# Multiplying the input product by the norm's token scale after PSUM instead of before it

## The chip, the cores and the metric

One core of a Trainium2 chip. The time is the device time of one launch in microseconds (us), as the median of several runs; smaller is better. The engines work side by side, each through its own queue in order: TensorE (matmul; "PE" in the profile, "PEld" its weight loads), VectorE ("DVE"), ScalarE ("ACT"), GpSimd ("POOL") and the DMA queues of SyncE ("SPq"), ScalarE ("ACTq") and GpSimd ("POOLq").

## The reference

One layer of an encoder over a sequence of 1024 tokens of 1024 features, all fp32. Its first lines are what the change touches:

```
h = x * rsqrt(mean(x * x, over features) + 1e-6) * norm1_w     # RMS norm of each token
z = h @ w_in                                                   # 1024 x 1024 by 1024 x 4528
c_q, c_kv, k_r, gdn_qkv, ga_f, ga_b, gb_f, gb_b, gdn_gate, gate_a, gate_b = split(z)
```

From z come: a latent attention (c_q and c_kv are normed again and multiplied up to queries, keys and values), a gated delta rule in both directions (gdn_qkv passes a convolution over five neighbouring tokens and a silu; the decays are exponentials of ga and gb), and three sets of gates (silu or sigmoid of z). Then follow the merge of both branches, an output product, a second norm, a squared-ReLU MLP and a last norm.

The rsqrt of the norm is one number per token. Multiplying a token's row of x by it, or that token's column of the product by it, gives the same z.

## The kernel before

Everything is held transposed: features lie on the 128 partitions, tokens along the free dimension, 1024 of them. x is eight tiles of 128 x 1024 (xt[0] to xt[7]), and z comes in 36 tiles of 128 features x 1024 tokens, one for each block w_in[i]. Tiles 0 to 3 are the keys (step k of the code), 4 is a mix of small columns (m), 5 to 8 the values (v), 9 to 11 the latents (c), 12 to 15 the queries (q), and 16 to 35 the gates (g).

A product at full precision is done in three matmul passes on split operands. A number is split into a high part (rounded to the type fp32r) and a low part (the rest); the passes are high x high, high x low and low x high. `split` makes both parts of a tile of x (a cast on ScalarE, a subtraction on VectorE or GpSimd); `wtile` loads a block of weights and does the same (L146 the load, L148 the cast, L150 the subtraction). `mm3` issues the 48 matmuls of one z tile: for each of the eight tiles of x the passes high x high and high x low in two halves of 512 tokens, then the eight of low x high. All matmuls of these helpers have line L157.

The prologue (L207 to L258) runs so. Weight blocks 0 and 1 and x are loaded by SyncE's queue; VectorE multiplies the two blocks by norm1_w (L221). TensorE forms z tiles 0 and 1 from the plain fp32 operands, 16 fp32 matmuls each, which the profile shows as 32 records; K0 orders them by the arrival of x. ScalarE squares the tiles of x (L230), VectorE adds the squares up (L232), TensorE sums them over the partitions with a matrix of ones (L237, at high priority), and `rsqrt` makes the token scale r1 from it on ScalarE and VectorE (L187 to L192). VectorE multiplies tiles 0 and 1 by r1 while it copies them out of PSUM (L247). Then, for each k, VectorE forms x * norm1_w * r1 (L251), ScalarE casts it (L170) and VectorE or GpSimd subtracts (L171); these pairs, xs, are what the other 34 tiles are formed from.

`z_tile(i)` gives tile i in PSUM, and each step takes it from there: `conv_tile` (the steps k, v and q) multiplies and adds five shifted copies on VectorE (L277), for k straight out of PSUM, for v and q out of a copy that ScalarE makes (L270); step m and `lora_norm` copy it with ScalarE; step g applies silu or sigmoid on ScalarE (L533) and stores the result to memory with ScalarE's DMA queue (L534).

PSUM has two buffers of 128 x 1024 (psA: z tiles, the Q, K and projection products) and four of 128 x 512 (psB). SBUF units are counted: 35 large ones ("u"; the names mem.alloc), 5 for passing work ("f"; fill.alloc), three raw weight buffers, four for split weights.

The string ORDER gives the order of the steps in the program. A scheduler of the framework then orders each engine's instructions: by their place in the program, with an instruction that must wait letting a later one go ahead, all by estimated durations. The semaphores follow from it; on the chip each engine runs its list in order. The i steps of ORDER are sixteen parts of a triangular inverse on VectorE (L519 multiplies, L521 adds, each on the result of the one before); what they give is stored by SyncE (L525) and read in the z steps (L655, L661) near the end of ORDER. Q steps (L584 multiplies a product out of PSUM) stand between the gates. After ORDER comes the scan of the delta rule: its states are loaded (L707, L708), and its exponentials run on ScalarE (L754), used first at L757.

Of the kernel before, what the change touches and what calls it, by code (L numbers as in the profile page):

```python
# [46 lines left out]
K0 = 6  # L47
# [50 lines left out]
def block_kernel(ctx: ExitStack, tc: tile.TileContext, xT, pos, cpar, gpar, w_in, w_uq, w_ukv,  # L98
# [108 lines left out]
    w0, xt = [], []  # L207
    nw = par[:, N1:N1 + 8]
    for k in range(8):
        if k < 2:  # L210
            raw = wp.tile([128, 1024], F32, tag="wraw", name=f"wi{k}_r", bufs=3)
            w0.append(raw)
            w3, src = (x.rearrange("p (k c) -> p k c", k=8) for x in (raw, w_in[k]))
            parts = (slice(0, 2), slice(2, 8))
            nc.sync.dma_start(w3[:, parts[0]], src[:, parts[0]])
        xt.append(mem.alloc())
        nc.sync.dma_start(xt[k].ap, xT[k * 128:(k + 1) * 128, :])
        if k < 2:
            nc.sync.dma_start(w3[:, parts[1]], src[:, parts[1]])
            for ks in parts:  # L220
                V.tensor_tensor(w3[:, ks], w3[:, ks], bc(nw[:, ks], 128), ALU.mult)  # L221
    pz = [pa("ps_z0"), pa("ps_z1")]
    for i, k in [(i, k) for k in range(K0) for i in range(2)] + \
            [(i, k) for i in range(2) for k in range(K0, 8)]:
        mm_pass(pz[i], w0[i][:, k * 128:(k + 1) * 128], xt[k].ap, k == 0, k == 7)
    psn = [pb("ps_n1a"), pb("ps_n1b")]
    acc = fill.alloc()
    for k in range(8):
        sq = acc if k == 0 else fill.alloc()
        last = A.activation(sq.ap, xt[k].ap, AF.Square)  # L230
        if 0 < k < 7:
            V.tensor_tensor(acc.ap, acc.ap, sq.ap, ALU.add)  # L232
            sq.free()
    with tc.high_priority(1000):
        for i, t in enumerate((acc, sq)):
            for sl, ps in zip(HS, psn):
                T.matmul(ps, ones, t.ap[:, sl], start=i == 0, stop=i == 1)  # L237
    acc.free()
    sq.free()
    r1 = fill.alloc()  # L240
    for i in range(2):
        rsqrt(r1.ap[:, HS[i]], psn[i], 1.0 / D, eps_t[:, 0:1], half("m"), half("t"),
              None if i else last)
    zb = big("ZB")
    zb = [zb[:, 0:1024], zb[:, 1024:2048]]
    for ps, z in zip(pz, zb):
        V.tensor_tensor(z, ps, r1.ap, ALU.mult)  # L247
    xs = []
    for k in range(8):
        xn = fill.alloc()  # L250
        V.scalar_tensor_tensor(xn.ap, xt[k].ap, pcol(N1 + k), r1.ap, ALU.mult, ALU.mult)  # L251
        h, l = mem.pair()
        split(h, l, xn.ap, G if k % 2 else V)
        xn.free()
        xs.append((h, l))

    def z_tile(i):
        if i < 2:  # L258
            return zb[i]
# [3 lines left out]
        return ps  # L263

    def conv_tile(dst, i, ch, slow=False):

        z = z_tile(i)
        if slow:
            zt = fill.alloc()
            A.copy(zt.ap, z)  # L270
            z = zt.ap
# [7 lines left out]
        if slow:  # L279
            zt.free()  # L280
# [23 lines left out]
    def s_k(h):  # L304
# [7 lines left out]
        if h == 1:  # L312
            r1.free()
            for t in xt:
                t.free()
# [4 lines left out]
    def s_m(_):  # L320
        ps = z_tile(4)
        zm.append(mem.alloc())
        A.copy(zm[0].ap, ps)
        G.dma_start(d_misc, zm[0].ap[0:16, :])
# [174 lines left out]
    def s_v(h):  # L499
        vT[h] = mem.alloc()  # L500
        conv_tile(vT[h].ap, 5 + h, 8 + h, slow=True)
# [28 lines left out]
    def s_g(i):  # L530
        ps = z_tile(16 + i)
        t = fill.alloc()
        late[0] = A.activation(t.ap, ps, AF.Silu if i < 4 else AF.Sigmoid)  # L533
# [9 lines left out]
    def lora_norm(z0, count, dim, wcol, name):  # L543
        tiles = []
        for i in range(count):
            pz_ = z_tile(z0 + i)
            t = fill.alloc()
            A.copy(t.ap, pz_)
# [139 lines left out]
    def s_q(h):  # L688
        qT[h] = mem.alloc()
        late[0] = conv_tile(qT[h].ap, 12 + h, h, slow=True)  # L690
# [9 lines left out]
    for h, l in xs:  # L700
        h.free()
        l.free()

# [832 lines left out]
```

## Time and profile before

| what | us |
|---|---|
| median of 3 runs | 1686.58 |
| lowest, highest | 1681.42, 1687.2 |
| the profiled execution, its own time | 1683.32 |
| its span | 1681.5 |
| TensorE matmul busy, share of the span | 1608.4 (96%) |
| VectorE busy | 1231.5 (73%) |
| ScalarE busy | 815.3 (48%) |
| GpSimd busy | 224.3 (13%) |
| TensorE's mean granted clock, share of full speed | 0.984 |

The profile is of one execution; its times count from the start of the span. "Idle before" an instruction, with a releaser behind an arrow, says how long the engine had nothing to do and what ended that. A name like u<-f,u gives the tile written and the tiles read, without buffer numbers; wi_r, wi_h and wi_l are the raw, the high and the low part of a block of w_in.

### The profile page before, as it was taken

The numbers are of one execution on the slowest core, as the hardware profiler recorded it, in microseconds if no ns is written. First come the engines' busy times: TensorE is split into PE (matmuls) and PEld (weight loads), VectorE is DVE, ScalarE is ACT, GpSimd is POOL, SyncE is SP. The second block draws the span as 40 slices with busy tenths as digits, with TensorE's granted clock in tenths as the row PEclk, the third lists the DMA queues.
The fourth block names the chain that finished last, engine by engine and source line by source line (L and its number), as shares of the span: only waits on it lengthen the run. The fifth ranks groups of instructions, "written<-read, shape, count | busy, mean of one in ns | idle before, by whom it ended". The sixth has DMA issues, their size and how long they took to land.

```text
span 1681.5 us, 21862 instructions
## 1 busy us (share of the span) xinstructions
PE 1608.4 (96%) x8177; PEld 1324.0 (79%) x8177; DVE 1231.5 (73%) x1823; ACT 815.3 (48%) x1393; POOL 224.3 (13%) x247
## 2 busy tenths in 40 slices
PE   8899999999989889999999998999999889999997
PEld 3687788878768878888878886888888657888886
DVE  6987999931345678888787568677776699888766
ACT  5567431441335557878762335444444443444333
POOL 1212100000004445555300000000000000000012
PEclk9999999999989999999999999999999999999999
DMA  4135243472234252101173212443443454444213
GB/s 184 58 108 135 79 160 114 137 213 88 76 101 132 74 159 76 51 26 39 55 245 113 101 38 81 150 151 138 168 152 141 154 208 143 154 161 154 83 57 101
DMA packets 87545, 200.00 MB, mean 119 GB/s; under 512 B 20224, under 2 KB 37888, under 8 KB 87184
## 3 DMA queue, kind: packets, MB, share of 16 engines
q1 hardware_dynamic: 63840, 158.14, 28.3%
q10 hardware_dynamic: 22784, 36.97, 6.4%
q0 software_dynamic: 816, 3.51, 1.0%
q8 instruction: 64, 1.05, 0.3%
q14 instruction: 41, 0.34, 0.1%
HBM read 136.79 MB, written 61.80 MB: 118 GB/s over the span
## 4 chain that ended last, share of the span: by engine, by line
PE 77%; DVE 10%; DMA 5%; ACT 5%; issue 2%; POOL 1%; ACTq 0%; SPq 0%; DVEq 0%; POOLq 0%
PE ps_z L157 15%; PE ps_af L1200 10%; PE ps_ay L1200 9%; PE ps_cf L1200 5%; PE ps_w L157 5%; PE ps_p L157 5%; PE ps_s L849 5%; PE ps_cy L1200 4%; PE ps_pv L891 3%; PE ps_pt L872 3%; PE ps_df L1200 3%; PE ps_y L1440 2%; PE ps_dy L1200 2%; DMA f<-d_vl 2%; DVE u L277 1%
## 5 line engine op out<-in xcount | busy, mean ns | idle before, releaser
L157 PE MATMUL ps_z<-u,wi_h 128*128 128x512 f32 x1088 | 260.9, 396 | 10.5 <-POOL u L171 1.7
L157 PEld LDWEIGHTS ps_z<-u,wi_h 128*128 128x128 f32 x1088 | 204.7, 190 | 57.7 <-ACT u L170 3.9
L1200 PE MATMUL ps_af<-u,f_w 128*128 128x512 f32 x768 | 181.9, 389 | 0.0
L1200 PE MATMUL ps_ay<-u,y_w 128*128 128x512 f32 x672 | 168.2, 396 | 8.7 <-ACT y_w L1188 3.1
L1200 PEld LDWEIGHTS ps_af<-u,f_w 128*128 128x128 f32 x768 | 144.0, 188 | 30.2 <-ACT u L1241 0.4
L1200 PEld LDWEIGHTS ps_ay<-u,y_w 128*128 128x128 f32 x672 | 125.8, 189 | 42.2 <-ACT y_w L1188 5.9
L157 PE MATMUL ps_z<-u,wi_l 128*128 128x512 f32 x544 | 133.5, 395 | 0.0
L1448 POOL TENSOR_TENSOR u<-u,q 128x256 f32<-128x256 f32 x20 | 16.2, 809 | 828.0 <-ACT q L1447 827.7
L157 PEld LDWEIGHTS ps_z<-u,wi_l 128*128 128x128 f32 x544 | 102.7, 190 | 21.6
L849 PE MATMUL ps_s<-u,u 128*128 128x512 f32 x384 | 105.9, 409 | 3.5 <-ACT u L837 2.4
L1200 PE MATMUL ps_cf<-u,f_w 128*128 128x512 f32 x384 | 94.7, 397 | 5.7 <-ACT f_w L1188 5.7
L150 DVE TENSOR_TENSOR wi_l<-wi_r,wi_h 128x1024 fp32r<-128x1024 f32 x34 | 41.5, 1220 | 77.3 <-PE ps_z L157 61.3
L852 DVE TENSOR_REDUCE sx<-ps_s 128x1 f32<-128x1024 f32 x64 | 77.9, 1218 | 21.3 <-PE ps_s L849 19.9
L1200 PE MATMUL ps_cy<-u,y_w 128*128 128x512 f32 x336 | 86.1, 394 | 6.7 <-DVE y_w L1189 6.2
L1200 PEld LDWEIGHTS ps_cf<-u,f_w 128*128 128x128 f32 x384 | 73.6, 192 | 22.0 <-ACT f_w L1188 6.5
L854 ACT ACTIVATE u<-ps_s,sx 128x1024 f32<-128x1024 f32 x64 | 72.2, 1128 | 31.9 <-DVE sx L852 31.5
L148 ACT CAST wi_h<-wi_r 128x1024 fp32r<-128x1024 f32 x34 | 35.7, 1050 | 104.0 <-PE ps_z L157 89.3
L878 DVE TENSOR_TENSOR u<-ps_pt,u 128x512 fp32r<-128x512 f32 x128 | 82.3, 679 | 5.1 <-ACT u L877 5.1
L856 POOL TENSOR_SCALAR u<-u,sx 128x1024 f32<-128x1024 f32 x64 | 72.0, 1128 | 84.9 <-DVE sx L855 82.0
L1200 PEld LDWEIGHTS ps_cy<-u,y_w 128*128 128x128 f32 x336 | 62.8, 189 | 22.9 <-DVE y_w L1189 8.3
L849 PEld LDWEIGHTS ps_s<-u,u 128*128 128x128 f32 x384 | 68.2, 191 | 15.3 <-ACT u L837 2.8
L1189 DVE TENSOR_TENSOR f_w<-f_r,f_w 128x512 fp32r<-128x512 f32 x48 | 33.1, 690 | 56.6 <-ACT f_w L1188 56.6
(368 smaller groups left out, 3262.1 us busy)
## 6 DMA issues: line engine op xcount, KB each, us to landing
u<-d_u SPq DMA_DIRECT2D x42, 512.0 KB, 4.3
wi_r<-w_in SPq DMA_DIRECT2D x34, 512.0 KB, 3.5
f_r<-w_ff SPq DMA_DIRECT2D x32, 512.0 KB, 3.3
d_u<-u SPq DMA_DIRECT2D x28, 512.0 KB, 4.0
d_z<-f ACTq DMA_DIRECT2D x20, 512.0 KB, 3.2
f<-d_z SPq DMA_DIRECT2D x20, 512.0 KB, 4.3
y_r<-w_ff SPq DMA_DIRECT2D x18, 512.0 KB, 3.9
d_u<-u ACTq DMA_DIRECT2D x16, 512.0 KB, 2.6
```

Of the source, the lines that this page charges most:

```text
L148: A.copy(hi, raw)
L150: V.tensor_tensor(lo, raw, hi.bitcast(F32), ALU.subtract)
L157: T.matmul(ps[:, sl], w, x[:, sl], start=start, stop=stop)
L849: T.matmul(pss[:, sl], a.r[:, qsl], b.r[:, sl], start=i == 0, stop=i == 2)
L852: V.tensor_reduce(sx[:, 0:1], pss, AX.X, ALU.max, negate=True)
L854: A.activation(P.ap, pss, AF.Exp, bias=sx[:, 0:1], accum_out=sx[:, 1:2])
L856: G.tensor_scalar(P.ap, P.ap, sx[:, 1:2], 1.0, ALU.mult, ALU.mult)
L872: T.transpose(pt[:, k * 128:(k + 1) * 128], P.ap[:, ko:ko + 128], ident)
L878: V.tensor_tensor(lv, p3, hf_, ALU.subtract)
L891: T.matmul(pso[:, 0:256], VC[kb].r[:, h * 128:(h + 1) * 128], PT[kg][i].r[:, k * 256:(k + 1) * 256], start=kb == 0 and i == 0, stop=kb == ...
L1200: T.matmul(ps, w[:, a, k * 128:(k + 1) * 128], self.xops[k][i].parts[b], start=n == 0 and i in FIRST, stop=n == 3 * self.g - 1, skip_group ...
L1440: T.matmul(ps[:, 0:n], w[:, o:o + 128], x[:, sl], start=j + k == 0, stop=j == 2 and k == 3)
```

## The change

The token scale r1 leaves the operands. x is split as x * norm1_w: ScalarE makes the high part in one scaled copy, VectorE the low part in one multiply-and-subtract, straight from each loaded tile (the first two in halves). All 36 tiles, also 0 to 2, are formed in split passes; for tiles 0 to 2 the three passes are issued one after the other. The norm's sum is formed behind tile 1. `z_scaled` multiplies every tile by r1 on VectorE on its way out of PSUM, in one instruction (tiles 0 to 2: in two halves; tile 2 lies in two psB buffers). So `conv_tile` always works on an SBUF copy, and step g applies its activation to that copy in place. ScalarE's squares are held behind the casts (that of tile k behind the cast of tile k + 4, at most 7). The order of loads becomes w_in[0], x, w_in[1]. r1 is held in a large unit until the end of ORDER; the tiles of x are let go after their squares.

```
--- before.py
+++ after.py
@@ -44,7 +44,6 @@
 
 ORDER = "kkkmrvGGklGtvSvvGsciiSigiigcSSgiQigQQiiQgQgQigQgiQqgigoggiKVKVViKgigogigzzqggzqKqzggV"
 PIECES = tuple((i, i + 256) for i in range(0, S, 256))
-K0 = 6
 LEAD, LAG = 3, 2
 VS, VS2 = (3, 4), (0, 1)
 HQ = 0
@@ -204,71 +203,84 @@
 
 
 
-    w0, xt = [], []
-    nw = par[:, N1:N1 + 8]
+    def wraw(src, name):
+        raw = wp.tile([128, 1024], F32, tag="wraw", name=f"{name}_r", bufs=3)
+        nc.sync.dma_start(raw, src)
+        return raw
+
+    xt, xs = [], []
+    w0 = wraw(w_in[0], "wi0")
     for k in range(8):
-        if k < 2:
-            raw = wp.tile([128, 1024], F32, tag="wraw", name=f"wi{k}_r", bufs=3)
-            w0.append(raw)
-            w3, src = (x.rearrange("p (k c) -> p k c", k=8) for x in (raw, w_in[k]))
-            parts = (slice(0, 2), slice(2, 8))
-            nc.sync.dma_start(w3[:, parts[0]], src[:, parts[0]])
         xt.append(mem.alloc())
         nc.sync.dma_start(xt[k].ap, xT[k * 128:(k + 1) * 128, :])
-        if k < 2:
-            nc.sync.dma_start(w3[:, parts[1]], src[:, parts[1]])
-            for ks in parts:
-                V.tensor_tensor(w3[:, ks], w3[:, ks], bc(nw[:, ks], 128), ALU.mult)
-    pz = [pa("ps_z0"), pa("ps_z1")]
-    for i, k in [(i, k) for k in range(K0) for i in range(2)] + \
-            [(i, k) for i in range(2) for k in range(K0, 8)]:
-        mm_pass(pz[i], w0[i][:, k * 128:(k + 1) * 128], xt[k].ap, k == 0, k == 7)
-    psn = [pb("ps_n1a"), pb("ps_n1b")]
+    w1 = wraw(w_in[1], "wi1")
+
+    def wsplit(raw, name):
+        hi = wp.tile([128, 1024], F32R, tag="ws", name=f"{name}_h", bufs=4)
+        A.copy(hi, raw)
+        lo = wp.tile([128, 1024], F32R, tag="ws", name=f"{name}_l", bufs=4)
+        V.tensor_tensor(lo, raw, hi.bitcast(F32), ALU.subtract)
+        return hi, lo
+
+    early, casts = [wsplit(w0, "wi0")], []
+    for k in range(8):
+        h, l = mem.pair()
+        for sl in (HS if k < 2 else [slice(0, 1024)]):
+            cast = A.activation(h.r[:, sl], xt[k].ap[:, sl], AF.Copy, scale=pcol(N1 + k))
+            V.scalar_tensor_tensor(l.r[:, sl], xt[k].ap[:, sl], pcol(N1 + k), h.ap[:, sl],
+                                   ALU.mult, ALU.subtract)
+        xs.append((h, l))
+        casts.append(cast)
+    early.append(wsplit(w1, "wi1"))
     acc = fill.alloc()
     for k in range(8):
         sq = acc if k == 0 else fill.alloc()
         last = A.activation(sq.ap, xt[k].ap, AF.Square)
+        tc.add_manual_dep(last.ins, casts[min(k + 4, 7)].ins.name, nosync, reason="order")
+        xt[k].free()
         if 0 < k < 7:
             V.tensor_tensor(acc.ap, acc.ap, sq.ap, ALU.add)
             sq.free()
-    with tc.high_priority(1000):
-        for i, t in enumerate((acc, sq)):
-            for sl, ps in zip(HS, psn):
-                T.matmul(ps, ones, t.ap[:, sl], start=i == 0, stop=i == 1)
-    acc.free()
-    sq.free()
-    r1 = fill.alloc()
-    for i in range(2):
-        rsqrt(r1.ap[:, HS[i]], psn[i], 1.0 / D, eps_t[:, 0:1], half("m"), half("t"),
-              None if i else last)
-    zb = big("ZB")
-    zb = [zb[:, 0:1024], zb[:, 1024:2048]]
-    for ps, z in zip(pz, zb):
-        V.tensor_tensor(z, ps, r1.ap, ALU.mult)
-    xs = []
-    for k in range(8):
-        xn = fill.alloc()
-        V.scalar_tensor_tensor(xn.ap, xt[k].ap, pcol(N1 + k), r1.ap, ALU.mult, ALU.mult)
-        h, l = mem.pair()
-        split(h, l, xn.ap, G if k % 2 else V)
-        xn.free()
-        xs.append((h, l))
+    r1 = mem.alloc()
+    pz = []
+    for i in range(3):
+        w = early[i] if i < 2 else wtile(w_in[i], f"wi{i}")
+        ps = [pa(f"ps_z{i}")] if i < 2 else [pb(f"ps_z{i}a"), pb(f"ps_z{i}b")]
+        pz.append([ps[0][:, 0:HALF], ps[0][:, HALF:2 * HALF]] if i < 2 else ps)
+        for p, q in ((0, 0), (0, 1), (1, 0)):
+            for k in range(8):
+                for s, sl in enumerate(HS):
+                    T.matmul(pz[i][s], w[p][:, k * 128:(k + 1) * 128], xs[k][q].r[:, sl],
+                             start=p + q + k == 0, stop=p == 1 and k == 7)
+        if i == 1:
+            psn = [pb("ps_n1a"), pb("ps_n1b")]
+            for j, t in enumerate((acc, sq)):
+                for sl, ps in zip(HS, psn):
+                    T.matmul(ps, ones, t.ap[:, sl], start=j == 0, stop=j == 1)
+            acc.free()
+            sq.free()
+            for j in range(2):
+                rsqrt(r1.ap[:, HS[j]], psn[j], 1.0 / D, eps_t[:, 0:1], half("m"), half("t"),
+                      None if j else last)
 
     def z_tile(i):
-        if i < 2:
-            return zb[i]
+
+        if i < 3:
+            return zip(HS, pz[i])
         w = wtile(w_in[i], f"wi{i}")
         ps = pa(f"ps_z{i}")
         mm3(ps, w, 0, xs)
-        return ps
-
-    def conv_tile(dst, i, ch, slow=False):
-
-        z = z_tile(i)
-        if slow:
-            zt = fill.alloc()
-            A.copy(zt.ap, z)
-            z = zt.ap
+        return [(slice(0, 1024), ps)]
+
+    def z_scaled(dst, i):
+        for sl, ps in z_tile(i):
+            V.tensor_tensor(dst[:, sl], ps, r1.ap[:, sl], ALU.mult)
+
+    def conv_tile(dst, i, ch):
+
+        zt = fill.alloc()
+        z = zt.ap
+        z_scaled(z, i)
         c = CW + ch * 5
         A.activation(dst, z, AF.Copy, scale=pcol(c + 2))
         for t in (0, 1, 3, 4):
@@ -276,8 +288,7 @@
             d0, d1 = max(0, -o), S - max(0, o)
             V.scalar_tensor_tensor(dst[:, d0:d1], z[:, d0 + o:d1 + o], pcol(c + t),
                                    dst[:, d0:d1], ALU.mult, ALU.add)
-        if slow:
-            zt.free()
+        zt.free()
         return A.activation(dst, dst, AF.Silu)
 
 
@@ -309,18 +320,13 @@
                                accum_out=kn[:, h * N + n:h * N + n + 1])
         t.free()
         kn_last[:] = [ins]
-        if h == 1:
-            r1.free()
-            for t in xt:
-                t.free()
 
 
     zm, d_misc = [], dr.tile([16, 1024], F32, name="d_misc")
 
     def s_m(_):
-        ps = z_tile(4)
         zm.append(mem.alloc())
-        A.copy(zm[0].ap, ps)
+        z_scaled(zm[0].ap, 4)
         G.dma_start(d_misc, zm[0].ap[0:16, :])
 
 
@@ -498,7 +504,7 @@
 
     def s_v(h):
         vT[h] = mem.alloc()
-        conv_tile(vT[h].ap, 5 + h, 8 + h, slow=True)
+        conv_tile(vT[h].ap, 5 + h, 8 + h)
 
     def s_S(h):
         stack(vT[h], h, d_vs).free()
@@ -528,9 +534,9 @@
     d_z = dr.tile([20, 128, 1024], F32, name="d_z")
 
     def s_g(i):
-        ps = z_tile(16 + i)
         t = fill.alloc()
-        late[0] = A.activation(t.ap, ps, AF.Silu if i < 4 else AF.Sigmoid)
+        z_scaled(t.ap, 16 + i)
+        late[0] = A.activation(t.ap, t.ap, AF.Silu if i < 4 else AF.Sigmoid)
         A.dma_start(d_z[i], t.ap)
         t.free()
 
@@ -543,9 +549,8 @@
     def lora_norm(z0, count, dim, wcol, name):
         tiles = []
         for i in range(count):
-            pz_ = z_tile(z0 + i)
             t = fill.alloc()
-            A.copy(t.ap, pz_)
+            z_scaled(t.ap, z0 + i)
             tiles.append(t)
         ps = pa(name)
         for i, t in enumerate(tiles):
@@ -687,7 +692,7 @@
             mem.live -= 1
     def s_q(h):
         qT[h] = mem.alloc()
-        late[0] = conv_tile(qT[h].ap, 12 + h, h, slow=True)
+        late[0] = conv_tile(qT[h].ap, 12 + h, h)
 
     steps = {"k": s_k, "m": s_m, "l": s_l, "r": s_r, "G": s_G, "s": s_s, "t": s_t, "v": s_v,
              "S": s_S, "i": s_i, "g": s_g, "c": s_c, "Q": s_Q, "K": s_K, "V": s_V, "o": s_o,
@@ -700,6 +705,7 @@
     for h, l in xs:
         h.free()
         l.free()
+    r1.free()
 
 
     KST, VST = [mem.alloc() for _ in range(H)], [mem.alloc() for _ in range(H)]
```

## Rows read from the trace of the kernel before

**Rows 1.** The profile's page, busy share of each engine.

```profile
PE 1608.4 (96%) x8177; PEld 1324.0 (79%) x8177; DVE 1231.5 (73%) x1823; ACT 815.3 (48%) x1393; POOL 224.3 (13%) x247
```

**Rows 2.** Busy time (instructions) by engine and stretch; granted clock, DMA share, GB/s.

```profile
42.00:55.00 13.00, 9.84 (x34) 6.85 (x33) 13.00 (x9) 6.27 (x6) 7.23 (x3) 0.87 0.04 16
61.00:187.00 126.00, 122.71 (x587) 100.09 (x586) 105.59 (x119) 80.74 (x154) 27.04 (x29) 1.00 0.36 104
187.00:345.00 158.00, 155.60 (x689) 127.57 (x688) 154.66 (x173) 60.40 (x62) 1.03 (x2) 1.00 0.38 132
...
484.00:531.00 47.00, 42.28 (x268) 33.84 (x267) 16.47 (x15) 17.11 (x28) 4.75 (x6) 0.85 0.57 173
```

**Rows 3.** TensorE in order of time: start, us, line, operation, [idle before].

```profile
6.42 15.42 PE L157 MATMUL ps_z<-u,wi_r 128*128 128x512 f32 x30 [6.42 <-DMA u<-xT]
...
25.11 14.75 PE L157 MATMUL ps_z<-u,wi_r 128*128 128x512 f32 x34
...
57.54 3.83 PE L157 MATMUL ps_z<-u,wi_l 128*128 128x512 f32 x16
61.21 4.92 PE L157 MATMUL ps_z<-u,wi_h 128*128 128x512 f32 x21
...
72.65 7.53 PE L157 MATMUL ps_z<-u,wi_h 128*128 128x512 f32 x32 [1.12 <-DVE u L277]
...
112.14 1.17 PE L157 MATMUL ps_z<-u,wi_h 128*128 128x512 f32 x4 [1.19 <-DVE u L361]
```

**Rows 4.** ScalarE and VectorE in order of time, from the norm's sum to r1.

```profile
24.45 0.69 ACT L187 ACTIVATE f<-ps_n1a,eps_t 128x512 f32<-128x512 f32 x1 [2.75 <-PE ps_n1a L237]
...
29.98 0.69 DVE L192 SCALAR_TENSOR_TENSOR f<-t,f 128x512 f32<-128x512 f32 x1
```

**Rows 5.** A line: count, min/median/max ns, first and last start, shape.

```profile
L247 DVE TENSOR_TENSOR ZB<-ps_z,f x2: 1210/1210/1211, 39.8 to 45.4; 128x1024 f32<-128x1024 f32 x2
...
L533 ACT ACTIVATE f<-ps_z x20: 1023/1029/1031, 190.8 to 523.2; 128x1024 f32<-128x1024 f32 x20
...
L277 DVE SCALAR_TENSOR_TENSOR u<-ps_z,par,u x8: 1266/1276/1283, 66.3 to 110.7; 128x1022 f32<-128x1022 f32 x4, 128x1023 f32<-128x1023 f32 x4
```

**Rows 6.** TensorE and VectorE: a z tile, a Q tile, the next.

```profile
254.03 7.42 PE L157 MATMUL ps_z<-u,wi_h 128*128 128x512 f32 x32
...
264.91 1.98 PE L157 MATMUL ps_q<-u,wq_h 128*128 128x512 f32 x8
...
267.63 7.42 PE L157 MATMUL ps_z<-u,wi_h 128*128 128x512 f32 x32
...
255.65 1.22 DVE L584 TENSOR_TENSOR f<-ps_q,u 128x1024 f32<-128x1024 f32 x1
```

**Rows 7.** ScalarE in order of time, squares of the last two tiles of x.

```profile
17.01 1.06 ACT L230 ACTIVATE f<-u 128x1024 f32<-128x1024 f32 x1 [0.21 <-DMA u<-xT]
18.29 1.06 ACT L230 ACTIVATE f<-u 128x1024 f32<-128x1024 f32 x1 [0.22 <-DMA u<-xT]
```

**Rows 8.** The stretches again, instructions that write or read ps_z alone.

```profile
61.00:187.00 126.00, 105.85 (x458) 84.95 (x457) 10.20 (x8) 9.30 (x9) 1.00 0.36 104
187.00:345.00 158.00, 131.03 (x573) 107.11 (x572) 0.00 (x0) 13.35 (x13) 1.00 0.38 132
```

**Rows 9.** The same of line L519 alone.

```profile
187.00:345.00 158.00, 52.99 (x62) 1.00 0.38 132
```

**Rows 10.** VectorE and TensorE, the inverse's end and first reader.

```profile
344.78 0.22 DVE L521 TENSOR_TENSOR SY<-SY,f 128x62 f32<-128x62 f32 x1
...
407.42 0.24 PE L661 MATMUL ptz<-ident,f 64*64 64x64 f32 x1
```

**Rows 11.** ScalarE and VectorE, the scan's first exponentials and their first use.

```profile
527.03 2.44 ACT L754 ACTIVATE f<-f,st 128x128 f32<-128x128 f32 x8
...
531.08 0.68 DVE L757 TENSOR_TENSOR f<-f,u 128x512 f32<-128x512 f32 x1
```

**Rows 12.** TensorE in order of time, behind the late load.

```profile
498.14 0.47 PE L662 MATMUL ptz<-ident,f 64*64 64x64 f32 x2 [4.72 <-DMA f<-d_x]
```

## The prediction

> **What bounds the kernel now.** The busy shares come first: TensorE matmul 96%, VectorE 73%, ScalarE 48% [rows 1]. So a change pays only where TensorE stands idle or works longer than it must. The table by stretches says where: from 61 us to 345 us TensorE is busy 122.7 of 126 us and 155.6 of 158, but from 42 to 55 us it is busy 9.84 of 13 while VectorE is busy all 13, and from 484 to 531 us 42.28 of 47 [rows 2]. The third view is TensorE's own order of time [rows 3]. The reader sees there the prologue: z tiles 0 and 1 as plain fp32 matmuls (wi_r) from 6.42 us to 39.9 us, with the norm's sum between them (ps_n1), and tile 2, the first split one (wi_h, wi_l), whose last pass starts only at 57.54. The split rows of x are what it waits for: they need the token scale r1, ready at 30.7 us [rows 4], and then eight multiplies, eight casts and eight subtractions, half of these on GpSimd. Last, the costs of one operation of each kind [rows 5].
>
> The sum is made against the profiled execution, 1683.3 us (span 1681.5, and 1.8 around it). The median shown, 1686.6, is 3.3 us higher; I add that at the end.
>
> **The prologue, before.** One split z tile takes 10.88 us (254.03 to 264.91) [rows 6]: 48 matmuls of 0.227. The fp32 tiles have 64 records: 34 of them take 14.75 us, 0.434 each, so a tile of 32 takes 13.9; the first 30 took 15.42 [rows 3], 2.4 more than at that pace. That is the engine's slow start. Tile 2's last pass begins at 57.54 and the tile after it goes on at 61.21 with 21 of its 32 wi_h matmuls [rows 3], so 11 had been run while tile 2 waited: 11 x 0.227 = 2.5 us, and tile 2 ends "in effect" at 58.7 us.
>
> **The prologue, after.** Loads: 512 KB land every 1.28 us, and the tenth 512 KB (two weight tiles, eight of x) is there at 18.29 [rows 7]. The order becomes w0, eight of x, w1: the last tile of x is there at 17.0, the first at about 8.0 (seven loads earlier), w1 at 18.3. ScalarE casts each tile of x as it lands, about as long as a square, 1.06 us [rows 7], under the 1.28 us of a load. But squares are let in behind the fifth cast: if three of them go ahead of the last cast, that ends at about 17.0 + 1.1 + 3 x 1.06 less what idles between, 20.7; if none does, 18.1. VectorE's low part is of the kind of L277, 1.28 us [rows 5], again as fast as a load, so the last is there at 19.4 to 22.0. TensorE starts when half of x's first tile is cast, 8.6 us. Six matmuls per tile of x are 1.36 us, so it nearly keeps step with the loads. I let it pay the slow start of 2.4 us again: by its own work tile 0 would end at 8.6 + 10.88 + 2.4 = 21.9, by its data 0.9 us (four matmuls) after the last low part, 20.3 to 22.9. I take 22.9, since ScalarE's order has squares between casts. Tile 1 follows, its weights long there: 33.8. The norm's sum is 3.3 us as now (21.84 to 25.11 [rows 3]) and stands behind tile 1: 37.1. Tile 2: 48.0 us. Against 58.7 that is 10.7 us: 6.0 us less matmul work (2 x (13.9 - 10.88)) and 4.7 us of idle time, net of a start that is 2.2 us later. Bounds: tile 0 at 20.3 (no square ahead, little of the slow start) gives 13.3; tile 0 at 27.9 (its three passes run strictly as written, the second and third after the last tile of x) gives 5.7.
>
> **What is late next.** r1 comes 6.2 us after the sum's first half (24.45 to 30.67 [rows 4]): about 43 us. Tile 0's PSUM is then read in two halves, 1.4 us, and free at 45; the tile after tile 2 needs that buffer at 48.0. Three us of cover; at the fast bound it stays, as both move together.
>
> **Evictions.** All 36 z tiles now leave PSUM by a VectorE multiply, 1.21 us [rows 5]; two did already. Twelve copies on ScalarE go, and 20 gate activations (1.03 us) stay but read SBUF [rows 5]; ScalarE is far from its limit, no gain there. On VectorE: until 187 us, 458 records of split matmuls over 48 from 61 us on and the three first tiles give some 12 to 13 evictions, 15 us, two of which are there already. VectorE idles 20 us from 61 to 187 [rows 2, 8], so they fit, if tightly. From 187 to 345 us there are 12 (573 over 48), 14.5 us, and only 3.3 idle [rows 2, 8]. But what fills VectorE here is the triangular inverse, L519 at 53 us [rows 9] and L521, its twin: a serial filler that nobody needs until its result is read. Its last operation starts at 344.78, and the first matmul on the result at 407.42 [rows 10]. Of these 62 us 11 are used up (14.5 less 3.3), or 26 if all from before 187 come on top. So the cost is not the 14.5 us but TensorE's wait for the buffer. In seven places a z tile is followed by a Q tile of 2.72 us (264.91 to 267.63) and then by a z tile that wants the buffer of the former [rows 6]. ScalarE freed it in 1.03 us. VectorE starts its own Q eviction 1.6 us after the Q tile ended (254.03, 255.65 [rows 6]), so a z eviction would end 1.6 + 1.21 = 2.8 us after its tile: 0.1 us late. Bounds: 0, and 7 x 1.3 = 9 us with one more instruction of 1.2 us ahead of each; I take 1.5, near the row.
>
> Two waits go: the 1.12 us before 72.65, and the 1.19 us before 112.14 (put down to L361, which is on VectorE too). In both, as I read them, TensorE waits for a buffer out of which VectorE's five-tap convolution reads its tile, four times 1.28 us [rows 3, 5]; now one multiply frees it. 2.3 us gained, between 0 and 3.3 (all that TensorE idles from 61 to 187 [rows 2]).
>
> **The end of the stage.** The last gate needs a multiply before its activation, and the scan's exponentials stand behind it on ScalarE, eight from 527.03 to 529.5; VectorE's first use is at 531.08 [rows 11]. That is 1.2 us later under 1.6 us of cover, so 0, and 1.2 if VectorE itself comes earlier. r1 holds one more large buffer until the stage ends, so one of the scan's eight state loads may start later; no row prices that, the nearest is a load's wait of 4.7 us [rows 12], and I take 0, since seven others go first.
>
> Sum: -10.7 - 2.3 + 1.5 = -11.5 us, 1671.8 for the profiled execution, 1675.1 as a median.
>
> **A rule against the change.** ScalarE moved a tile out of PSUM in 1.03 us, VectorE needs 1.21, and VectorE is the busier one [rows 1, 5]. The Trainium skill, TensorEngine Tiling (Array Packing), section PSUM Bottleneck, says to use both ScalarE and VectorE for emptying PSUM, and that this copy can become the limit; no run here shows it yet. By it the first rival would be the outcome.
>
> **The rivals.** (A) VectorE becomes the bound, slower. Place: the seven z-Q pairs. If an eviction stands behind half a step of the inverse (four instructions of 1.2 us) instead of behind one, TensorE waits 4.8 + 1.21 - 2.72 = 3.3 us each time, 23 us in all, against a gain of 13.0 (10.7 + 2.3): 10 slower, 1697. It decides from 3.4 us of queue ahead of each eviction (13.0 / 7 + 2.72 - 1.21), where the gain is just eaten up. For it: VectorE is busy 154.7 of 158 us [rows 2]. Against it: its Q evictions cut in after 1.6 us today [rows 6]. Chance 0.13.
> (B) The prologue gives little: the three passes run as written, or TensorE stays slow while x trickles in, and tile 0 ends near 28 us. Gain 5.7, less 1.2 at the end of the stage, and the two waits back: 4.5, 1682. Against it: while tile 2 waited, 11 matmuls of the next tile were run ahead of it [rows 3], so the order adapts. Chance 0.21.
> (C) More is gained: at 493.4 us TensorE waits 4.7 us for a load of the inverse's result [rows 12], and the stretch around it has a granted clock of 0.85 on average, that is, part of its 47 us at 1.2 instead of 2.4 GHz [rows 2]. The scan's state loads are issued in that stretch; with one large buffer less for them, and one ScalarE copy less ahead of it in that engine's queue, it may miss them: 4.7 us and half as much again or more for the slow part, about 8 us: 1667. It can as well collide elsewhere. Chance 0.16.
>
> **How the numbers follow.** The forecast, 1675, has 0.50, its own range 1670 to 1681. About 0.5% (8.4 us) is what a measurement here can tell from no change: faster means below 1678.2, slower above 1695.0. Of the forecast 0.36 lies below and 0.14 within; C adds 0.16 to faster, B 0.21 to the same, A is slower: 0.52, 0.35, 0.13. The range 1664 to 1690 takes in C and B and leaves A out.
>
> **What would show it.** Right: no fp32 matmuls of z, tile 2 done near 48 us, the two waits at 72 and 112 gone, VectorE with 33 multiplies of 1.21 us and six of half the size, z-Q pairs without idle time. Wrong: idle time of TensorE released by the new multiplies of more than a few us between 187 and 345 us (A), or tile 0 still running at 28 us (B).

## The result, and the profile after

The change made the kernel slower: median 1697.05 us (1696.15 to 1704.07, 5 runs) against 1686.53 (1681.42 to 1687.2, 5 runs), ratio 1.0077 with the 95% interval 1.0055 to 1.0098. The forecast was 1675.1, and 1697 lies above its range of 1664 to 1690. The profiled execution is the slowest of the five, 1704.07 (span 1702.3), 7.0 above its own median; that of before was 3.2 below its median. So of the 20.8 us between the two traces some 10 are spread, and what follows rests on waits that also stand in the traces of the experiments.

The busy shares are nearly those of [rows 1]: VectorE +20.7 us, ScalarE -7.3, TensorE +6.4.

```profile
PE 1614.8 (95%) x8209; PEld 1338.9 (79%) x8209; DVE 1252.2 (74%) x1856; ACT 808.0 (47%) x1385; POOL 215.0 (13%) x243
```

The stretches that answer to [rows 2], and three smaller ones; the last three lines are the smaller ones in the kernel before:

```profile
42.00:55.00 13.00, 13.00 (x55) 10.07 (x55) 7.62 (x9) 6.82 (x10) 0.00 (x0) 1.00 0.11 40
61.00:187.00 126.00, 114.65 (x529) 94.14 (x528) 103.67 (x119) 74.22 (x146) 24.37 (x25) 0.95 0.34 95
187.00:345.00 158.00, 149.46 (x637) 121.09 (x636) 147.38 (x154) 46.79 (x50) 10.36 (x7) 0.97 0.34 118
...
40.00:80.00 40.00, 39.86 (x178) 31.58 (x177) 25.80 (x27) 21.48 (x53) 1.70 (x2) 1.00 0.25 79
80.00:112.00 32.00, 32.00 (x163) 27.05 (x161) 31.14 (x28) 13.47 (x30) 3.88 (x6) 1.00 0.24 70
112.00:150.00 38.00, 28.37 (x122) 23.38 (x122) 22.39 (x46) 21.56 (x43) 8.51 (x12) 0.82 0.28 87
...
40.00:80.00 40.00, 34.07 (x144) 26.54 (x145) 37.78 (x29) 20.25 (x48) 11.85 (x5) 0.96 0.19 63
80.00:112.00 32.00, 30.28 (x153) 25.16 (x151) 30.37 (x29) 17.90 (x38) 6.44 (x7) 1.00 0.40 116
112.00:150.00 38.00, 37.59 (x189) 31.16 (x190) 25.85 (x46) 28.03 (x51) 8.98 (x12) 1.00 0.27 79
```

From 42 to 55 us TensorE is busy all the time now; the prologue did get shorter. The loss is behind it: 61 to 187 us went from 122.7 busy to 114.65, and the place is 112 to 150, where TensorE runs 28.37 of 38 us at a granted clock of 0.82 (37.59 at 1.00 before). VectorE idles 14.2 of the 40 us from 40 to 80, where it was busy 37.78 before, and is full from 80 to 112. It was nearly full there before too (30.37 of 32): what is new is that the work of the first stretch comes later, and the multiplies come on top.

TensorE in order of time answers to [rows 3]; the last lines are its long waits up to the scan.

```profile
8.27 2.81 PE L253 MATMUL ps_z<-u,wi_h 128*128 128x512 f32 x4 [8.27 <-ACT u L229]
...
18.94 10.00 PE L253 MATMUL ps_z<-u,wi_h 128*128 128x512 f32 x36 [3.80 <-ACT wi_h L220]
...
28.78 3.79 PE L253 MATMUL ps_z<-u,wi_l 128*128 128x512 f32 x16
...
54.46 1.75 PE L156 MATMUL ps_z<-u,wi_h 128*128 128x512 f32 x7
...
114.47 1.97 PE L309 MATMUL ps_st<-ident,u 128*128 128x128 f32 x8 [2.26 <-ACT u L292]
...
122.70 7.54 PE L156 MATMUL ps_z<-u,wi_h 128*128 128x512 f32 x32 [2.10 <-DVE f L277]
...
139.14 0.42 PE L379 MATMUL ps_r<-ident,rk 128*64 128x128 f32 x1 [5.27 <-DVE rk L377]
...
203.82 2.50 PE L156 MATMUL ps_z<-u,wi_l 128*128 128x512 f32 x5 [5.86 <-DVE wi_l L149]
```

The stretch just behind the wait at 139.14:

```profile
140.00:144.00 4.00, 4.00 (x15) 2.86 (x14) 1.21 (x6) 0.28 (x1) 1.53 (x4) 0.50 0.36 124
```

Tile 2 ends at 54.46, against 58.7 "in effect" before: 4.2 us gained. The waits of 1.1 and 1.2 us at 72 and 112 us are gone [rows 3]. At 139.14 TensorE has waited 5.27 us for the key scales (rk), and what it runs next is slow: from 140 to 144 us it is busy all the time and gets through 15 matmuls, at a granted clock of 0.50, that is, at 1.2 instead of 2.4 GHz. At 203.82 it has waited 5.86 us for a weight tile's low part.

Where the 5.27 us come from is read from VectorE and ScalarE in order of time, followed back from the key scales:

```profile
48.73 0.69 DVE L191 SCALAR_TENSOR_TENSOR u<-t,u 128x512 f32<-128x512 f32 x1
...
57.54 1.28 DVE L277 TENSOR_TENSOR f<-ps_z,u 128x512 f32<-128x512 f32 x2
63.55 2.60 DVE L289 SCALAR_TENSOR_TENSOR u<-f,par,u 128x1022 f32<-128x1022 f32 x2 [4.72 <-ACT u L285]
...
70.49 0.69 DVE L277 TENSOR_TENSOR f<-ps_z2a,u 128x512 f32<-128x512 f32 x1
...
113.36 1.06 ACT L292 ACTIVATE u<-u 128x1024 f32<-128x1024 f32 x1
...
123.31 0.33 ACTq L446 DMA_DIRECT2D d_rt<-u  x1
...
125.25 0.54 ACTq L311 DMA_DIRECT2D d_ks<-f  x1
...
131.84 0.31 ACT L319 ACTIVATE f<-f 128x128 f32<-128x128 f32 x1 [2.45 <-DMA d_ks<-f]
```

The same in the kernel before: a store of the rope step, the fourth key's silu, the store of its stack.

```profile
107.94 0.33 ACTq L440 DMA_DIRECT2D d_rt<-u  x1
...
113.37 1.06 ACT L281 ACTIVATE u<-u 128x1024 f32<-128x1024 f32 x1
...
116.36 0.33 ACTq L300 DMA_DIRECT2D d_ks<-f  x1
```

r1 is complete at 49.4 us, and tile 1 has been waiting in PSUM since 40. Its multiply starts at 57.54, tile 2's at 70.49, 16 us after TensorE left that tile. A key's multiply stands inside the key's step: VectorE runs one convolution, waits for ScalarE's copy that opens the next (4.72 us), and only then brings the next tile out. From 78 us on the convolutions of the third key, a value and the fourth key stand in VectorE's queue between the instructions of the rope step (some 19.5 us, L426 to L445). The fourth key's silu starts at 113.36; the store of its stack is issued at 125.25, behind two stores of the rope step in ScalarE's queue, its squares begin at 131.84, and rk is written at 138.90.

The lines of before say what of this is new. The fourth key itself is not late: its silu starts at 113.37 there. The rope step is: its stores go out at 107.94 before and at 123.31 after. In the changed kernel the key's store stands behind them in ScalarE's queue, 8.9 us later than before (125.25 against 116.36), and rk follows, 11.7 us later (127.18 before). No run changes the order of these stores alone, so how much of the 11.7 us is the order and how much VectorE's load stays open.

### The profile page after: what moved, and what is told of

Its sections match the earlier page's. It is cut to its first block, busy times and chain, and to the rows that moved or that the text cites. A ratio compares the mean times of both kernels' runs of the same rounds, so it can differ in the third digit from the quotient of the medians.

```text
span 1702.3 us, 21992 instructions
## 1 busy us (share of the span) xinstructions
PE 1614.8 (95%) x8209; PEld 1338.9 (79%) x8209; DVE 1252.2 (74%) x1856; ACT 808.0 (47%) x1385; POOL 215.0 (13%) x243
## 4 chain that ended last, share of the span: by engine, by line
PE 74%; DVE 10%; DMA 6%; ACT 5%; issue 2%; POOL 2%; SPq 0%; ACTq 0%; DVEq 0%; POOLq 0%
PE ps_z L156 12%; PE ps_af L1206 10%; PE ps_ay L1206 8%; PE ps_cf L1206 5%; PE ps_w L156 5%; PE ps_p L156 5%; PE ps_s L855 5%; PE ps_cy L1206 4%; PE ps_pv L897 3%; PE ps_pt L878 3%; PE ps_df L1206 3%; PE ps_y L1446 2%; PE ps_dy L1206 2%; DMA f<-d_vl 1%; DVE u L289 1%
## 5 line engine op out<-in xcount | busy, mean ns | idle before, releaser
L156 PE MATMUL ps_z<-u,wi_h 128*128 128x512 f32 x1056 | 251.7, 394 | 2.8 <-DVE f L277 2.4
L156 PEld LDWEIGHTS ps_z<-u,wi_h 128*128 128x128 f32 x1056 | 198.2, 189 | 47.1 <-issue 4.8
L277 DVE TENSOR_TENSOR f<-ps_z,u 128x1024 f32<-128x1024 f32 (+1 forms) x36 | 41.7, 1160 | 53.4 <-PE ps_z L156 53.2
```

Of the source, the lines that this page charges most:

```text
L156: T.matmul(ps[:, sl], w, x[:, sl], start=start, stop=stop)
L277: V.tensor_tensor(dst[:, sl], ps, r1.ap[:, sl], ALU.mult)
```

## The experiments

Theory M: what VectorE was given (the multiplies) and where they stand in its queue makes the steps ahead of the key scales late, and TensorE's own queue, in order, meets the end of that chain at ps_r and at a weight's low part. Rival P: r1 comes later than before (49.4 instead of 30.7 us) and by itself makes the rest late. A third reading goes with every run: the framework orders all queues anew for each kernel, so an edit is tested together with the order that came with it. All ratios are to the kernel before, run on the same chip beside it.

| kernel | median us | ratio, 95% interval | TensorE's ps_kq starts, us |
|---|---|---|---|
| before | 1686.5 | 1 | 524.4 |
| after | 1697.1 | 1.0077 [1.0055, 1.0098] | 538.4 |
| e1_no_mult | 1688.3 | 1.0010 [0.9996, 1.0023] | 530.4 |
| e2_before_mult | 1705.2 | 1.0106 [1.0089, 1.0123] | 538.8 |
| e3_w1_late | 1700.8 | 1.0082 [1.0062, 1.0101] | 532.4 |
| e4_rope_late | 1703.9 | 1.0088 [1.0059, 1.0118] | 537.6 |
| f1_evict_early | 1690.7 | 1.0016 [0.9999, 1.0033] | 521.9 |
| f2_rope_early | 1697.2 | 1.0060 [1.0039, 1.0081] | 529.9 |
| f3_gate_buf | 1705.2 | 1.0119 [1.0094, 1.0145] | 537.8 |
| f4_all | 1691.1 | 1.0033 [1.0015, 1.0050] | 526.7 |
| g1_evict_rope | 1684.9 | 0.9977 [0.9966, 0.9989] | 519.3 |
| g2_evict_rope_w1 | 1685.2 | 0.9977 [0.9961, 0.9993] | 520.5 |
| g3_evict_w1 | 1687.9 | 0.9992 [0.9979, 1.0005] | 520.0 |
| g4_gates_direct | 1693.6 | 1.0032 [1.0018, 1.0045] | 536.2 |

The last column, from each kernel's one profiled execution, is the end of the stage that holds the change. Such an execution can lie well off its kernel's median: f1's is the fastest of its ten, 8.5 us below.

**e1, the multiplies out of the changed kernel.**

```
-            V.tensor_tensor(dst[:, sl], ps, r1.ap[:, sl], ALU.mult)
+            if i < 3:
+                V.tensor_tensor(dst[:, sl], ps, r1.ap[:, sl], ALU.mult)
+            else:
+                A.copy(dst[:, sl], ps)
...
-        z_scaled(t.ap, 16 + i)
-        late[0] = A.activation(t.ap, t.ap, AF.Silu if i < 4 else AF.Sigmoid)
+        (_, ps), = z_tile(16 + i)
+        late[0] = A.activation(t.ap, ps, AF.Silu if i < 4 else AF.Sigmoid)
```

> The changed kernel, but tiles 3 to 35 leave PSUM as they did before: ScalarE copies, gates activated straight out of PSUM. The token scale is left out of these tiles (tiles 0 to 2 keep their multiply, so the keys still wait for r1). Theory M (the multiplies on VectorE make its chain of small steps late, and TensorE queues behind that chain twice, at 134 to 139 us and at 198 to 204 us): both waits go, and what is left is the prologue's gain of 4 to 7 us: 1680 to 1684 us. Rival P (r1 at 49.4 instead of 30.7 us starts the keys and all that follows late, whatever empties PSUM): the two waits stay, 1692 to 1698 us.

1688.3, between the two forecasts: the multiplies of tiles 3 to 35 carry about nine tenths of the loss, 0.67 of 0.77%. ps_r starts at 127.2 us, as in the kernel before (127.7) and 12 us earlier than in the changed kernel; the key's store goes out at 115.01 here, ahead of the rope's (120.70). But TensorE comes to ps_r early and waits there 7.8 us, longer than with the multiplies, so the rest of the change is no gain: what the prologue won is spent at this wait. That much of P stands.

**e2, the multiplies into the kernel before** (by a tile of ones, tiles 2 to 35).

```
-            A.copy(zt.ap, z)
+            V.tensor_tensor(zt.ap, z, one.ap, ALU.mult)
...
```

> The kernel before, with one thing of the change: every z tile from 2 on leaves PSUM through a VectorE multiply (by a tile of ones, so nothing else moves), gates activated in SBUF. Theory M: the waits at the decay step and at the inverse's start appear here too, 1698 to 1706 us. Rival P: the prologue is the old one, so at most the 0 to 3 us of single waits for a buffer, 1686 to 1690 us.

1705.2, 18 us slower with r1 as early as ever. That is M without P, but not at ps_r, which starts at 133.1 us without a wait. TensorE's longest wait stands later, from 173 to 181 us, where a multiply is behind the mask step s (L480 to L482) in VectorE's queue; from 61 to 187 us TensorE is busy 112.58 us, where the kernel before has 122.71:

```profile
61.00:187.00 126.00, 112.58 (x524) 91.38 (x523) 112.40 (x128) 67.79 (x138) 33.84 (x29) 0.93 0.35 98
...
180.66 1.62 PE L157 MATMUL ps_z<-u,wi_h 128*128 128x512 f32 x3 [7.75 <-DVE f L552]
...
177.02 2.36 DVE L482 TENSOR_TENSOR SY<-SY,sv 128x1024 f32<-128x1024 f32 x2
179.29 1.23 DVE L552 TENSOR_TENSOR f<-ps_z,u 128x1024 f32<-128x1024 f32 x1
```

**e3, the second weight's cast behind the last cast of x.**

```
+        if casts:
+            tc.add_manual_dep(ins.ins, casts[-1].ins.name, nosync, reason="order")
```

> The changed kernel with the cast of the second weight block ordered behind the last cast of x on ScalarE (it now stands ahead of the sixth cast and waits 4.0 us for its load there). TensorE's wait of 3.8 us at 15.1 us goes or shrinks, tile 2 ends 3 to 4 us earlier. Theory M: the later waits are set by VectorE's load, not by where TensorE stands, so the 3 to 4 us are lost again at the decay step: 1694 to 1698 us, no gain beyond 2 us. Rival P: everything comes 3 to 4 us earlier: 1693 us.

No gain; 1700.8 lies above both forecasts. The 3.80 us ahead of 18.94 are gone, and tile 2 comes no earlier:

```profile
18.25 1.22 PE L256 MATMUL ps_z<-u,wi_h 128*128 128x512 f32 x2 [0.76 <-ACT u L232]
20.23 7.13 PE L256 MATMUL ps_z<-u,wi_h 128*128 128x512 f32 x18 [0.76 <-ACT u L232]
27.20 3.79 PE L256 MATMUL ps_z<-u,wi_l 128*128 128x512 f32 x16
```

Two matmuls per tile of x, every 2 us (a cast and a square on ScalarE), and the low-part pass only behind the first pass: tile 0 ends at 31.0. In the changed kernel the wait for the cast had only stood where these gaps stand.

**e4, the rope step behind the decay step.**

```
-ORDER = "kkkmrvGGklGtv..."
+ORDER = "kkkmvGGklGrtv..."
```

> The changed kernel with the rotary step r (some 25 us of VectorE work) moved in the order of steps from ahead of the decay step l to behind it. Theory M in its stricter form (the l chain is late because multiplies, convolutions and the rotary step share VectorE, full from 80 to 120 us): l's chain ends some 10 us earlier against TensorE, the wait of 5.3 us at 134 us goes, the inverse starts earlier and the wait at 198 us shrinks: 1680 to 1688 us. Rival P: l is late because the keys are late, rotary step or not: 1694 to 1698 us.

(The r is the rope step.) The ps_r wait went (ps_r starts at 115.8), which M forecast and P did not, and waits came elsewhere: 8.6 us at the stack transposes (ps_st, for ScalarE's silu) and 8.0 us for one multiply. This move of the load gains nothing, and 1703.9 fits neither forecast.

**f1, the evictions of tiles 0 to 2 directly behind r1.**

```
+    zt3 = [fill.alloc() for _ in range(3)]
+    for i in range(3):
+        for sl, ps in zip(HS, pz[i]):
+            V.tensor_tensor(zt3[i].ap[:, sl], ps, r1.ap[:, sl], ALU.mult)
...
-        zt = fill.alloc()
+        zt = zt3[i] if i < 3 else fill.alloc()
```

> The changed kernel with one thing moved: the three multiplies that bring tiles 0 to 2 out of PSUM stand right behind the norm's scale, ahead of the convolution of the first key, each into its own buffer of the pool of five. Nothing else differs. Theory M (the multiplies that VectorE got lengthen the chain convolution, squares of k, r, l that TensorE's queue waits for at ps_r): VectorE uses some of the 13 us that it idles in 40 to 80 us, the rope and the conversions in 80 to 120 us come earlier, the wait at ps_r (5.3 us) shrinks by 2 to 5 us and the median comes to 1692 to 1695 against 1697 unmoved. Rival P (what is late is the norm's scale r1 itself, at 49.4 us, and everything behind it follows): no change beyond 1 us, 1696 to 1698. A third way: three buffers of the pool held from 50 us take them from the stacks of k; then ps_st waits grow and the time is 1698 to 1702.

1690.7: 0.61 of the 0.77% come back (6.4 us between the medians) by the place of three multiplies alone, with r1 as late as in the changed kernel. The stretches and tile 2's multiply:

```profile
40.00:80.00 40.00, 40.00 (x182) 31.80 (x181) 31.37 (x33) 23.07 (x56) 1.70 (x2) 1.00 0.27 87
80.00:112.00 32.00, 28.95 (x144) 24.24 (x143) 31.20 (x29) 13.75 (x30) 6.29 (x7) 1.00 0.23 69
112.00:150.00 38.00, 35.65 (x168) 29.63 (x169) 26.91 (x48) 23.21 (x46) 8.64 (x12) 0.91 0.30 89
...
56.88 0.68 DVE L269 TENSOR_TENSOR f<-ps_z2a,u 128x512 f32<-128x512 f32 x1
...
110.55 0.33 ACTq L452 DMA_DIRECT2D d_rt<-u  x1
...
116.94 0.33 ACTq L317 DMA_DIRECT2D d_ks<-f  x1
```

Tile 2 leaves PSUM at 56.88 instead of 70.49, VectorE works 5.6 us more from 40 to 80, and TensorE 7.3 more from 112 to 150, though 3.0 less from 80 to 112; part of this is spread, as f1's trace is its fastest execution. The ps_r wait is gone: the rope's stores are out at 110.55, so the key's goes at 116.94, though its silu starts no earlier (113.21). A wait of 5.4 us for that silu (ps_st) stands at 114 in its place, while VectorE is still full from 80 to 112. As the whole account, P has failed here.

**f2, the rope step in the prologue, ahead of r1.**

```
+    s_r(0)
     r1 = mem.alloc()
-ORDER = "kkkmrvGGkl..."
+ORDER = "kkkmvGGkl..."
```

> The changed kernel with the rope tables' step (29 VectorE instructions, 19.5 us by the trace of the changed kernel) issued in the prologue ahead of r1, where VectorE idles 11.7 of 20 us in 30 to 50 us. The arithmetic is the same. Theory M: the 19.5 us leave the stretch 80 to 120 us in which VectorE is full; the third key's convolution ends some 10 us sooner, the store of its stack no longer waits behind the rope's stores on ScalarE's queue, the ps_r wait of 5.3 us and the 2.1 and 2.3 us waits ahead of it go, and the granted clock holds at 1.0 in 112 to 150 us. Expected 1688 to 1692, the rest of the loss being the wait behind affine_select at 204 us and the start of the scan. Rival P: r1 gets later by what the rope puts in front of its VectorE work (up to 3 us), and the time is 1697 to 1700.

The ps_r wait went, and TensorE was busy all of 112 to 150. But the time came down little if at all (1697.2; the intervals overlap): the mask step s (three 128x1024 multiplies for each quarter) now lies in VectorE's queue ahead of one eviction, as in e2, and one wait of 10.2 us shows it:

```profile
174.36 0.77 PE L156 MATMUL ps_z<-u,wi_h 128*128 128x512 f32 x1 [10.20 <-DVE f L314]
...
170.72 2.35 DVE L487 TENSOR_TENSOR SY<-SY,sv 128x1024 f32<-128x1024 f32 x2
173.00 1.21 DVE L314 TENSOR_TENSOR f<-ps_z,u 128x1024 f32<-128x1024 f32 x1
```

I expected 1688 to 1692 and had priced one wait, not what comes up behind it. The time is in P's range, and r1 is complete 4.8 us later here (54.2); but ps_r starts at 122.1, 17 us earlier than in the changed kernel, so the way there was not P's.

**f3, the last gate in a large buffer.**

```
-        t = fill.alloc()
+        t = (mem if i == 19 else fill).alloc()
```

> The changed kernel, but the last gate's tile takes a buffer of the large pool instead of one of the five that the scan's first tables wait for. If the start of the scan loses its 6 to 7 us because the last gate's multiply, activation and store hold that buffer (the store lands at 545 us and POOL and ScalarE wait 5.2 and 5.5 us for it), the first tables are loaded some 6 us sooner, the idle 3.6 us at ps_o goes and the time is 1691 to 1694. Rival: another buffer of the five (that of the last query's convolution or of the gate before) is released as late, or one fewer large buffer delays a load of the states by more than that: 1696 to 1700.

A miss, 8 us above the changed kernel's median. Five loads of the scan's tables (L749) now stand ahead of the loads of its states in SyncE's queue: the first of these goes out at 533.66 us, where the changed kernel had three out from 494.60 on. TensorE waits 4.3 us for them. That the gate's hold on a large buffer brought this order about is my reading; no run shows it apart.

```profile
505.94 27.63 SPq L749 DMA_DIRECT2D f<-d_vl  x5
533.66 0.46 SPq L713 DMA_DIRECT2D u<-d_vs  x1
```

**f4, f1 to f3 together; g1, f1 and f2 together; g2, g1 with e3's edit; g3, f1 with e3's edit.** Their diffs are those above.

> The three moves together (early evictions, rope in the prologue, the last gate in the large pool), the arithmetic unchanged. Theory M: the losses that the changed kernel's trace shows at 112 to 150 us (10 us) and at the scan's start (6 us) go and the prologue's 4.3 us stay; with the wait at 204 us (5.9 us) left, 1681 to 1688, at or below the 1687 of the kernel before. Rival P: the prologue's gain is eaten wherever the first wait of the key chain stands, 1690 to 1697.

> Early evictions and the rope step in the prologue together, without the change of the last gate's buffer, which by itself had cost 8 us. Theory M (place of the multiplies in VectorE's queue decides, moves add up): 1691 of all three moves less those 8 is 1683, below the 1687 of the kernel before. Rival: with the evictions early the 14 us of VectorE idle time are used already, the rope's move adds its ps_z waits as it did alone, and the time is 1690 to 1695.

> As the run with early evictions and early rope, and the second weight block's cast stands behind the last cast of x on ScalarE's queue. Theory M: the 3.8 us that TensorE waited for that cast go and now reach the end, since the key chain is no longer late: 2 to 4 us below that run, 1679 to 1682. Rival P': the time lost in the prologue is given back at a later wait, as it was when this edit stood alone: within 1.5 us of that run.

> Early evictions (1690.7 by themselves) with the second weight block's cast behind the last cast of x; the rope stays where it was. If VectorE's queue up to the third key's convolution was what swallowed the 3.8 us, they reach the end now: 1686 to 1688. If the wait at ps_st (5.4 us at 114 us, VectorE full of rope and convolution) is what TensorE meets whenever it comes, the wait grows by as much and the time stays at 1690 to 1692.

g1 is the first kernel faster than the one before, by 0.23% (0.11 to 0.34%), and g2, with the same two moves, repeats it. It takes the change and both moves in the order of work: neither move alone gave it. It does so with r1 complete only at 53.9 us, later than in the changed kernel, against P once more. No run puts the rope step early in the kernel before, so how much of the gain is the change's stays open. Its stretches show what f1 and f2 lacked, VectorE used from 40 to 80 and with room from 80 to 112, and TensorE without a gap from 80 to 150:

```profile
40.00:80.00 40.00, 37.35 (x160) 29.21 (x159) 39.30 (x39) 19.78 (x38) 4.22 (x2) 0.96 0.19 61
80.00:112.00 32.00, 32.00 (x167) 27.26 (x167) 22.41 (x30) 21.95 (x54) 3.93 (x6) 1.00 0.35 109
112.00:150.00 38.00, 38.00 (x190) 31.65 (x189) 29.50 (x43) 24.62 (x46) 11.29 (x15) 1.00 0.38 103
```

f4 is g1 plus f3's loss, with the same 4.3 us of waiting for state loads. g2 against g1 shows that the weight's cast is worth nothing, as e3 had; g3 against f1 is unclear, their intervals overlap.

**g4, the gates straight from PSUM** (without r1), the other tiles as in the change.

```
-        z_scaled(t.ap, 16 + i)
-        late[0] = A.activation(t.ap, t.ap, AF.Silu if i < 4 else AF.Sigmoid)
+        (_, ps), = z_tile(16 + i)
+        late[0] = A.activation(t.ap, ps, AF.Silu if i < 4 else AF.Sigmoid)
```

> The changed kernel, but the 20 gate tiles leave PSUM straight through ScalarE's activation as in the kernel before, so r1 is left out of the gates; the other 16 tiles keep their multiply. It splits theory M: the kernel without any multiply from tile 3 on took 1688. If the 20 gate multiplies (21 to 25 us of VectorE, and the last one ahead of the scan) carry the loss, 1688 to 1691. If the 16 early ones do, at the key chain and behind affine_select, with the scan's start 6 us earlier as the only gain: 1691 to 1694. If the gates' multiplies cost nothing: 1697.

1693.6 lies where the second reading, the 16 early multiplies, put it. Without the gates' multiplies 0.45 of the 0.77% is gone; e1, without the others as well, had 0.67. These shares and f1's 0.61 don't add up; as I read it they need not, since all go through the same VectorE queue. The wait at ps_r is unchanged (5.5 us) and ps_kq starts only 2 us earlier; the scan's opening is shorter: from the first ps_kq to the first matmul of the attention's scores (ps_s) it takes 87 us instead of 90, with 85 before.

## Why the prediction was wrong, point by point

**Evictions until 187 us: the step that failed.** It set 15 us of multiplies against 20 us of VectorE idle time from 61 to 187 and said "they fit, if tightly". The sum did fit: VectorE still idles 22 us there. But idle time is no stock. In the kernel before 12.2 of the 20 us lie from 112 to 150, behind the rope step and the last key's convolution, and 1.6 from 80 to 112, where they were needed; in the changed kernel 14.2 us lie from 40 to 80, most of it in waits for ScalarE. So the added instructions make what stands behind them in VectorE's queue late. In the changed kernel that is the rope step, whose stores hold the last key's store and with it ps_r, 11 us later than before; in e2 it is a multiply behind the mask step. e2 (10.1 us less TensorE work from 61 to 187 us, 18 us in all), e1 (ps_r back at 127.2 without the multiplies) and f1 show that the multiplies and their place cost this; the path through the stores is read from the traces. The prediction put the term at 0 and looked for the price from 187 us on. Part of the price is the clock: from 112 to 150 TensorE is idle 9.6 us and granted 0.82 on average, and 0.50 just behind the ps_r wait. The sum had no term for this either.

**Prologue, -10.7.** Measured -4.2. The start was right (8.27 against 8.6), and the pace was not: I let TensorE run six matmuls per tile of x. The three passes run as written, which was rival (B)'s condition: tile 0's last pass ends at 32.6 us (14 matmuls of tile 1 go ahead of it), and (B)'s gain of 5.7 is near. w1's cast, ahead of x's sixth on ScalarE, looks like the cause in the trace of after; e3 shows that it is not.

**Two buffer waits, -2.3.** Right: both are gone. It gained nothing on the whole, since a wait of 5.27 us came at 139.

**z-Q pairs, +1.5, and rival (A).** The term was too high, and (A) was wrong in its place: that its 1697 is the time that came is chance. Q tiles follow z tiles without a gap, and TensorE stands idle in that stretch elsewhere:

```profile
271.76 1.98 PE L156 MATMUL ps_q<-u,wq_h 128*128 128x512 f32 x8
...
274.48 7.42 PE L156 MATMUL ps_z<-u,wi_h 128*128 128x512 f32 x32
...
196.18 0.27 DVE L525 TENSOR_TENSOR f<-SY 128x62 f32<-128x62 f32 x1 [4.34 <-POOL SY L486]
...
379.08 0.22 DVE L527 TENSOR_TENSOR SY<-SY,f 128x62 f32<-128x62 f32 x1
...
425.71 0.24 PE L666 MATMUL ptz<-ident,f 64*64 64x64 f32 x1
```

At 196.18 VectorE has waited 4.34 us for GpSimd's mask, at the start of the inverse, and an eviction and the weight's low part that TensorE needs (at 202.54) stand behind it: the 5.86 us. No run took this wait alone away, so its own share stays open. The inverse, as the prediction said, took the added work: it ends 34 us later (379.1 against 344.8 [rows 10]), still 46 us ahead of its reader.

**End of the stage, 0.** Open. In this trace the scan's opening takes 5 us longer than before. The cover of 1.6 us was counted on ScalarE's exponentials; the wait here came through the buffer of the last gate, which a scan table takes over. Multiply, activation and store follow one another, and then GpSimd's mask, the next table and its exponential:

```profile
537.22 1.23 DVE L277 TENSOR_TENSOR f<-ps_z,u 128x1024 f32<-128x1024 f32 x1 [2.12 <-PE ps_z L156]
...
545.21 1.05 POOL L753 TENSOR_SCALAR_AFFINE_SELECT f<-f 128x512 f32<-128x512 f32 x1 [5.16 <-DMA d_z<-f]
...
551.15 0.63 ACT L751 ACTIVATE f<-f 128x512 f32<-128x512 f32 x1 [5.49 <-DMA f<-d_vl]
...
552.40 1.20 PE L820 MATMUL ps_o<-f,u 128*128 128x128 f32 x4 [3.62 <-ACT u L792]
```

g4, without the gates' multiplies, has the scan's opening back at 87 us; but f1, with all of them, has 87 too, and g1 91 with the gain it shows. So whether the multiply by itself sets the 5 us stays open: f3, meant to test the buffer alone, made the state loads late and settles nothing on it. State loads at 0 held for the change itself: one fewer was early, and no matmul waited for them.

**Rival (C).** The 4.7 us wait for the inverse's result [rows 12] did go (0.4 us now), but that was won only after more had been lost.

**The rule.** With VectorE alone bringing z tiles 2 to 35 out of PSUM, e2 lost 18 us. The Trainium skill, TensorEngine Tiling (Array Packing), section PSUM Bottleneck, says of array tiling that both ScalarE and VectorE should be used for emptying PSUM; e2's 18 us agree with it, though no array tiling is in play here. I had the rule in hand and priced it in the wrong stretch.

## What to carry to other kernels

Idle time of an engine is worth something only where the added work can stand: read it in slices that end where a chain ends, and ask which in-order queue of another engine meets that chain's end. Compare each step of the chain with the trace of before: here the key that TensorE waits for was on time, and a neighbour's store in ScalarE's queue was not. When an operation moves to another engine, look where the code emits it: three multiplies in another place gave back most of the loss here, and with one more step moved the loss became a gain of 0.2%. A wait that is taken away shows the next one; f2 and e4 removed the same 5 us and gained little or none of it.

## What was not expected

Waits of TensorE cost more than themselves here. From 112 to 150 us the changed kernel idles 9.6 us, in three waits of 2.3, 2.1 and 5.3, and the stretch has a granted clock of 0.82; g1, without a wait in the same stretch, has 1.00 and ran 190 matmuls there against 122, though not the same ones.
